# Value projection of a hybrid encoder block: the third group by seven block products, token blocks kept in place for the keys, and another order in the last row tile

## The chip, the cores and the metric

The kernel runs on one core of a Trainium2 chip, as one launch. Its time is the device time of an execution in microseconds (us); the median of the runs is compared. The engines are named as the profile names them: PE is the matrix engine (TensorE, with PEld for its weight loads), DVE the vector engine, ACT the scalar engine, POOL GpSimd, and SP the engine that issues most DMAs. ACT issues DMAs too.

## The reference

One sub-layer over 1024 tokens of 1024 channels. The input is normalised and multiplied by one wide weight matrix `w_in`; the products are the queries, keys and values of three mixers, gate paths and merge gates. The mixers' outputs are gated, projected, merged by sigmoid gates, projected once more, normalised and added to the input:

```python
h = rms_norm(x, g_pre[layer])
a_qkv, bq, bk, bv, mq, ga, gb, gm, mg = jnp.split(h @ w_in[layer], split_at, axis=-1)
a_qkv = a_qkv.reshape(b, s, 3, n_groups * A_HEADS, HEAD_DIM)
aq = rope(a_qkv[:, :, 0], pos)
ak = rope(a_qkv[:, :, 1], pos)
av = a_qkv[:, :, 2]
for gi, (window, dil) in enumerate(A_GROUPS):
    ...
out = merged @ w_out[layer]
x = x + rms_norm(out, g_post[layer])
```

`av` has 3 groups x 8 heads x 64 = 1536 columns, so each of the three value groups is a matrix product of 1024 tokens by 1024 channels by 512 columns. The keys `ak` have 1536 columns too. All of it is in float32.

## The kernel before

**Precision.** A float32 operand is split in two parts: a high part by an ACT copy into the matmul type (L105) and a low part by a DVE subtraction (L106), `split(dst_h, dst_l, src)`. A product is three matmuls: high by high, low by high, high by low. The tokens lie split in `hh` and `hl`, eight tiles of 128 channels by 1024 tokens.

**Seven block products.** Where a product can be cut into 2 x 2 blocks on both sides, the kernel takes the seven products of `PRODUCTS` in place of eight. A11, A12, A22 are blocks of weights and S1 to S4 sums and differences of them; B11, B21, B22 are blocks of tokens and T1 to T4 differences of those. T1 to T4 were formed earlier and lie unsplit in DRAM (`tsd`), four tiles of 128 x 512 each. What a product adds to which output is in the evacuation functions: S1 gives two outputs, A12 and A22 one each, the others go into running sums (`vv`, `vy`).

**The stage of the values.** Value groups VG[1] and VG[2] go together as one 1024 x 1024 x 1024 product. The loop has 28 steps, four for each of the seven products, and a step is four token tiles x three matmuls with 512 streamed columns. In a step n the loop writes down, in this order: the matmuls of n; the evacuation of one bank of the product before (`left`); the splits for step n+2 (`split_at`); sums of weights (`sum_at`); the stores of the evacuated bank; the token loads for step n+5 (`blocks_at`); and a stage of `operand`, another small job of three stages (loads, two DVE operations, a store). The third group, VG[0], follows in 16 steps of the same length as a plain product: for two token halves, eight channel tiles, four token tiles and three matmuls (the branch `i is None` at L1101). Its weights are loaded in four loads `wr<-in_wv`. During these 16 steps T1 to T4 are loaded once more from DRAM and split again, 16 tiles `kT`, for the keys. Each evacuated bank of 128 tokens x 512 columns is scaled by a column (`rcol`) and stored by ACT, operation and DMA issue (`v_store`, L948 and L949).

**The stage of the keys.** Six blocks of keys by the seven products each, 12 matmuls of 512 columns a product. The weights are loaded (`k_load`), their sums made on POOL (`k_sum`, L1039, into `sf`), and split (`k_own` for A11 and A12, `k_block` for the others, into `ch`).

**The last stage.** The output projection, again by seven products (L2019). Its last product's last bank, token tile 7, comes in two halves of 256 columns: each is summed with a running sum (L2105), squared with a row sum on ACT (L1993), added into a scalar per row (L2109) and weighted (L2110). The scalar is raised to a power on POOL (L2111), both halves of the row tile are finished (L2113) and stored by SP and ACT (L2114). `row(T)` finishes and stores another row tile (L2007, L2008).

**Order.** PE's order is written by hand in the whole kernel, and in these stages that of ACT, DVE, POOL and SP as well (`manual_schedule`): the instructions of an engine stand in the order in which the program writes them. A tile name with `bufs=n` has n places; a further tile of that name waits until the readers of the place that it takes are done.

## Time and profile before

| | us |
|---|---|
| median of 3 runs | 1418.86 (1418.45 to 1419.08) |
| the profiled execution | 1420.1 |
| its span, first to last instruction | 1418.3 |
| PE busy | 1393.4 |
| DVE busy | 1040.7 |
| ACT busy | 670.6 |
| third value group, first matmul | 538.04 |
| first matmul of the keys | 582.59 |

The mean granted clock of PE over the span is 0.998. In the profile, a row of the timeline gives the start in us from the start of the span, the duration, the engine, the line, the operation, what it writes and reads, and in brackets the idle time before it and what ended it. The duration of a matmul is longer than the distance between two of them, because they overlap; the distance is what PE needs for one. A group row gives the count, the busy time in us, the mean in ns, and idle time with what ended it. A row of the waits gives who waited for whom, the total in us, how often, and the longest. The chain is the work that ended last, followed back from the end.

### The profile page before, as it was taken

To read this page: it belongs to the slowest core of one execution; us is meant where nothing else is said; L and a number is where in the kernel's file an instruction comes from. 1 tells how busy PE (TensorE), PEld (TensorE's weight loads), DVE (VectorE), ACT (ScalarE), POOL (GpSimd) and SP (SyncE) were. 2 spreads that over 40 slices of the span, in tenths; PEclk is the share of its full clock that TensorE was granted. 3 is DMA by queue.
4 is the path that set the end of the run, shared out by engine and by line. 5 is a ranking of instruction groups with operands and counts; after the bars stand their busy time and mean duration, and the time that the engine had idled before them with its cause. 6 is when DMAs were issued, how large, how long until landed. Compare 5 with 4: busy or idle time off the path is not lost.

```text
span 1418.3 us, 21284 instructions
## 1 busy us (share of the span) xinstructions
PE 1393.4 (98%) x7496; PEld 1120.2 (79%) x7496; DVE 1040.7 (73%) x1830; ACT 670.6 (47%) x1425; POOL 505.1 (36%) x390
## 2 busy tenths in 40 slices
PE   7999999999999999999999999999999999999997
PEld 7899986656666888888888878787888888888886
DVE  7768677767773695688885777765888788677977
ACT  6544365665555445322146676656543434222232
POOL 0416703766666000432153353520433331034303
PEclk9999999999999999999999999999999999999999
DMA  6356532322210779544543554555353543856255
GB/s 238 108 166 220 182 119 71 112 82 79 75 57 23 260 225 298 162 166 178 193 131 106 129 162 116 140 140 182 106 150 126 178 171 124 321 217 212 93 199 178
DMA packets 122059, 219.67 MB, mean 155 GB/s; under 512 B 25504, under 2 KB 56032, under 8 KB 121952
## 3 DMA queue, kind: packets, MB, share of 16 engines
q1 hardware_dynamic: 95744, 187.60, 41.1%
q10 hardware_dynamic: 26208, 30.71, 6.1%
q8 instruction: 59, 0.97, 0.3%
q14 instruction: 48, 0.39, 0.1%
HBM read 152.88 MB, written 65.37 MB: 154 GB/s over the span
## 4 chain that ended last, share of the span: by engine, by line
PE 78%; DVE 6%; DMA 5%; ACT 5%; issue 3%; POOL 2%; SPq 1%; DVEq 0%; POOLq 0%; ACTq 0%
PE s L125 23%; PE sc L125 9%; PE d L143 6%; PE d L145 6%; PE d L147 6%; PE ov L803 4%; PE s L2019 3%; PE s L1101 3%; PE s L1385 2%; PE tr L1441 2%; PE s L788 2%; PE s L787 2%; PE tr L769 2%; DMA vrt<-rld 2%; PE d L544 2%
## 5 line engine op out<-in xcount | busy, mean ns | idle before, releaser
L143 PE MATMUL d<-hh,wh 128*128 128x512 f32 x480 | 194.9, 406 | 1.7 <-DVE fth L228 1.7
L145 PE MATMUL d<-hl,wh 128*128 128x512 f32 x480 | 194.1, 404 | 0.0
L147 PE MATMUL d<-hh,wl 128*128 128x512 f32 x480 | 190.7, 397 | 0.0
L794 POOL TENSOR_TENSOR bl<-bl,bp 128x512 f32<-128x512 f32 x96 | 130.7, 1362 | 54.4 <-ACT bp L790 49.0
L105 ACT ACTIVATE wh<-wr 128x512 fp32r<-128x512 f32 (+1 forms) x91 | 69.6, 772 | 133.0 <-PE sc L125 78.7
L125 PE MATMUL sc<-hh,wh 128*128 128x512 f32 x384 | 118.4, 389 | 0.0
L106 DVE TENSOR_TENSOR wl<-wr,wh 128x512 fp32r<-128x512 f32 (+1 forms) x63 | 78.9, 1265 | 50.6 <-ACT wh L105 50.6
L143 PEld LDWEIGHTS d<-hh,wh 128*128 128x128 f32 x480 | 90.3, 188 | 27.1 <-issue 6.3
L147 PEld LDWEIGHTS d<-hh,wl 128*128 128x128 f32 x480 | 90.5, 189 | 21.1 <-issue 4.7
L1398 ACT ACTIVATE pra<-pra,sts 128x192 f32<-128x192 f32 (+2 forms) x192 | 84.3, 442 | 47.9 <-DVE sts L1397 47.4
L145 PEld LDWEIGHTS d<-hl,wh 128*128 128x128 f32 x480 | 90.5, 189 | 19.2 <-issue 4.7
L790 ACT ACTIVATE bp<-s 128x512 f32<-128x512 f32 x128 | 75.7, 595 | 43.3 <-PE s L788 42.3
L770 DVE TENSOR_REDUCE bn<-tr 128x1 f32<-128x512 f32 x128 | 84.8, 683 | 12.7 <-PE tr L769 11.3
L106 DVE TENSOR_TENSOR ch<-sf,ch 128x512 fp32r<-128x512 f32 x68 | 55.9, 823 | 40.5 <-ACT ch L105 40.4
L125 PEld LDWEIGHTS sc<-hh,wh 128*128 128x128 f32 x384 | 72.1, 188 | 15.1
L105 ACT ACTIVATE ch<-sf 128x512 fp32r<-128x512 f32 x68 | 41.6, 628 | 89.3 <-PE s L125 46.4
L1249 DVE SCALAR_TENSOR_TENSOR t2a<-d,tab 32x512 f32<-32x512 f32 x96 | 66.0, 687 | 22.4 <-PE d L147 20.7
L1925 POOL TENSOR_TENSOR acc<-acc,th 128x1024 f32<-128x1024 f32 x15 | 41.3, 2756 | 109.9 <-DVE th L1924 109.9
L1039 POOL TENSOR_TENSOR sf<-wr 128x512 f32<-128x512 f32 x12 | 19.0, 1580 | 168.7 <-DMA wr<-in_wu 111.1
L1708 POOL TENSOR_TENSOR sf<-wr 128x512 f32<-128x512 f32 x22 | 28.8, 1329 | 130.4 <-DVE ch L106 81.7
L125 PE MATMUL sc<-hl,wh 128*128 128x512 f32 x192 | 74.7, 389 | 0.0
L1253 POOL TENSOR_TENSOR aq<-t1a,t2a 128x512 f32<-128x512 f32 x24 | 44.5, 1858 | 82.1 <-DVE t1a L1252 82.1
(444 smaller groups left out, 3773.9 us busy)
## 6 DMA issues: line engine op xcount, KB each, us to landing
wr<-in_wu SPq DMA_DIRECT2D x64, 512.0 KB
kd<-kr ACTq DMA_DIRECT2D x48, 256.0 KB
th<-thd SPq DMA_DIRECT2D x24, 512.0 KB
thd<-rs ACTq DMA_DIRECT2D x44, 256.0 KB
g2d<-fth SPq DMA_DIRECT2D x24, 256.0 KB
wos<-os SPq DMA_DIRECT2D x12, 512.0 KB
kraw<-kd SPq DMA_DIRECT2D x12, 512.0 KB
kswp<-kd SPq DMA_DIRECT2D x48, 128.0 KB
```

The costliest lines, as they stand in the source:

```text
L105: A.activation(dst_h, src, AF.Copy)
L106: V.tensor_tensor(dst_l, src, dst_h.bitcast(F32), op=OP.subtract)
L125: PE.matmul(out_ps, a, b, start=i == 0, stop=i == n - 1)
L143: PE.matmul(dst, wh[:, k, :], hh[k][:, t], start=k == 0, stop=False)
L145: PE.matmul(dst, wh[:, k, :], hl[k][:, t], start=False, stop=False)
L147: PE.matmul(dst, wl[:, k, :], hh[k][:, t], start=False, stop=k == 7)
L770: fp["last"] = V.tensor_reduce(st[i]["n"][:, j, c:c + 1], s, axis=AX.X, op=OP.min)
L790: A.activation(pp, s, AF.Exp, scale=-1.0)
L794: G.tensor_tensor(lsum[i % 2], lsum[i % 2], pp, op=OP.add)
L803: PE.matmul(o[e * 64:e * 64 + 64], VS[:, kt, kv], d.pop(kt), start=kt < 2, stop=kt >= NT - 2)
L1249: V.scalar_tensor_tensor(t2[i], p[j], -0.125, tab[1][j, t], op0=OP.mult, op1=OP.mult)
L1398: A.activation(src, src, AF.Exp, scale=-1.0, bias=bias, accum_out=sts[:, h, 1, T:T + 1])
```

## The change

The third group is computed by the seven products as well, cut into two halves of tokens, of channels and of columns. A matmul now streams 256 columns, two token tiles share one bank, and there are 28 steps of 12 matmuls. New functions load, sum, split, evacuate and store for it; a list `SIDE` says behind which step what is written down. A store covers 128 tokens x 256 columns, so a bank takes two of them.

The T tiles stay split through the third group and the keys: they are loaded into places of weight blocks that are done (`KT_PLACE`), the weight blocks are cut into tiles of two channel tiles each for that (`Rows`), and only two tiles of T3 are loaded and split a second time. Split weights have 2 places `sl` in place of 8 for weights and tokens together, beside `wh` and `wl`. Several tiles of the keys take places of the value stage by name.

In the last stage row 6 is finished and stored in two halves, behind the second sum of row 7's bank; the weighting of the second half moves behind the scalar.

```diff
     def split_at(i, k):
...
         if (i, k) not in SB:
-            SB[i, k] = wslot(k % 2) if i == 1 else slot()
+            SB[i, k] = wslot(k % 2 if i == 1 else 0) if i == 1 or k < 2 else slot()
...
+    KT_PLACE = {"T2": ["kT20", "kT21", "kT22", "kT23"], "T3": ["vA220", "vA221", "kT32", "kT33"],
+                "T1": ["vA110", "vA111", "vA210", "vA211"], "T4": ["vS20", "vS21", "vA120", "vA121"]}
 
     def kt_load(nm, k):
-        KT[nm, k] = tp.tile([P, 1024], R, name=f"k{nm}{k}")
+        KT[nm, k] = vb.tile([P, 1024], R, name=KT_PLACE[nm][k])
         nc.sync.dma_start(KT[nm, k][:, hi].bitcast(F32), tsd[int(nm[1]) - 1, k])
...
+    def v3_load(nm, t):
+        V3[nm] = t
+        u, kh = int(nm[1]) - 1, 4 * int(nm[2]) - 4
+        nc.sync.dma_start(t.rearrange("p (k f) -> p k f", k=4), wv[VG[0], :, kh:kh + 4, 256 * u:256 * u + 256])
+
+    def v3_sum(nm, a, b, op, t=None):
+        V3[nm] = V3[a] if t is None else t
+        V.tensor_tensor(V3[nm], V3[a], V3[b], op=op)
+
+    def v3_split(nm):
+        h, l = wslot(0), wslot(1)
+        split(h, l, V3[nm])
+        W3[nm] = [z.rearrange("p (k f) -> p k f", k=4) for z in (h, l)]
+
+    def v3_out(u, t, b, r):
+        for z in range(2):
+            T = 4 * t + 2 * b + z
+            x = r[:, half_cols[z]]
+            A.activation(x, x, AF.Copy, scale=rcol[:, T:T + 1])
+            nc.scalar.dma_start(vdr[VG[0], 2 * u:2 * u + 2, T * 128:T * 128 + 128].rearrange("p t f -> t p f"),
+                                x.rearrange("t (p f) -> t p f", p=2))
+
+    def v3_evac(i, b, ps_):
+        nm = PRODUCTS[i][0]
...
+        if nm == "A11":
+            return [lambda: A.activation(v3v[b], ps_, AF.Copy)]
+        if nm == "A12":
+            r = add(r3(), v3v[b])
+            return [lambda: v3_out(0, 0, b, r)]
+        if nm == "S1":
+            x, y = add(r3(), v3y[b]), add(v3v[b], v3v[b])
+            return [lambda: v3_out(1, 1, b, x), lambda: v3_out(0, 1, b, y)]
+        if nm == "A22":
+            y = add(v3y[b], v3y[b])
+            return [lambda: v3_out(1, 0, b, y)]
+        add((v3y if nm == "S3" else v3v)[b], v3v[b])
+        return []
...
+        if n in (16, 18):
+            v3_load(f"A1{2 if n == 16 else 1}", wp.tile([P, 1024], F32, name="wr", bufs=WR))
+        elif n in (21, 22):
+            v3_load(f"A2{n - 20}", vb.tile([P, 1024], F32, name=f"vS1{n - 21}"))
+        elif n == 24:
+            v3_split("A11")
+            kt_load("T3", 0)
+        elif n == 25:
+            v3_sum("S3", "A11", "A21", OP.subtract, V3["A21"])
+        elif n == 26:
+            v3_split("A12")
+            kt_load("T3", 1)
...
+    SIDE = {1: [lambda: operand(7, 1)],
+            2: [lambda: operand(7, 2), lambda: v3_sum("S2", "A22", "S3", OP.subtract, v3.tile([P, 1024], F32, name="xS2"))],
+            4: [lambda: v3_split("S2")], 5: [lambda: kt_split("T3", 0)], 6: [lambda: kt_split("T3", 1)],
+            8: [lambda: v3_split("S3")], 10: [lambda: v3_sum("S4", "A12", "S2", OP.subtract)], 12: [lambda: v3_split("S4")],
+            13: [lambda: k_load(0, 0)], 14: [lambda: v3_sum("S1", "A11", "S2", OP.add)], 16: [lambda: v3_split("S1")],
+            18: [lambda: k_load(0, 1)], 20: [lambda: v3_split("A22")], 23: [lambda: k_sum(0, 1)],
+            24: [lambda: k_own(0)], 25: [lambda: k_sum(0, 2)]}
+    for n in range(28):
+        i, k = divmod(n, 4)
+        an, bn = PRODUCTS[i]
+        if k == 0:
+            now = [pss1(), pss1()]
...
+        for j in range(4):
+            c = slice(j * 128, j * 128 + 128)
+            for q, (a, b) in enumerate(((bh[:, c], wh_[:, k]), (bl[:, c], wh_[:, k]), (bh[:, c], wl_[:, k]))):
+                PE.matmul(now[j // 2][:, half_cols[j % 2]], a, b, start=k == 0 and j % 2 == 0 and q == 0,
+                          stop=k == 3 and j % 2 == 1 and q == 2)
+        for _ in range(2 if n < 2 else 1):
+            for f in left.pop(0)() if left else []:
+                f()
...
+        for f in SIDE.get(n, ()):
+            f()
+        if k == 3:
+            left += [lambda i=i, b=b, z=now[b]: v3_evac(i, b, z) for b in range(2)]
 
     while left:
         for g in left.pop(0)():
             g()
...
     k_sum(0, 3)
     k_sum(0, 4)
     k_block(0, "S2")
     k_block(0, "S3")
...
-        if h == 0:
-            row(6)
+        if h:
+            row(6, (lo,))
+        else:
+            V.tensor_tensor(c11[3][:, e], vs[3][:, e], gp[:, e], op=OP.mult)
         V.scalar_tensor_tensor(r, q[:, 2 * h:2 * h + 1], 1.0 / D, r, op0=OP.mult, op1=OP.add)
-        V.tensor_tensor(c11[3][:, e], vs[3][:, e], gp[:, e], op=OP.mult)
+    V.tensor_tensor(c11[3][:, e], vs[3][:, e], gp[:, e], op=OP.mult)
+    row(6, (hi,))
     G.tensor_tensor(r, r, mhalf[:, 0:1], op=OP.pow)
```

More of the change, by code (lines that the diff above doesn't have):

```diff
@@ L1008, in kt_split @@
         split(h, l, l.bitcast(F32))
-    kt_all = [(nm, k) for nm in ("T2", "T3", "T1", "T4") for k in range(4)]
     KR = {}
@@ L1112, in block @@
             f()
[L1113 to L1120 removed]
+        if n < 23:
+            blocks_at(*divmod(n + 5, 4))
         for stage in (2, 1, 0):
@@ new lines, in block @@
+        if k == 3:
+            left += [lambda i=i, j=j, b=now[j]: v_evac(i, j, b) for j in range(4)]
+    SIDE = {1: [lambda: operand(7, 1)],
[5 more added lines that the diff above has]
+            24: [lambda: k_own(0)], 25: [lambda: k_sum(0, 2)]}
@@ L1157, in block @@
     kpp, kp = pool("kp")
-    kv_ = [kp.tile([P, 512], F32, name=f"kv{j}") for j in range(2)]
+    kv_ = [vb.tile([P, 512], F32, name=f"vv{2 + j}") for j in range(2)]
     for j in range(2):
```

117 lines of the change are left out of this document (52 added, 65 removed).

## The prediction

> **What bounds the kernel.** I read the page first, then TensorE's (PE's) waits from 455 to 600 us, the chain of waits there, and the timelines of the engines around the part that changes.
>
> ```profile
> span 1418.3 us, 21284 instructions
> ...
> PE 1393.4 (98%) x7496; PEld 1120.2 (79%) x7496; DVE 1040.7 (73%) x1830; ACT 670.6 (47%) x1425; POOL 505.1 (36%) x390
> ```
>
> ```profile
> PE s L1101 <- DVE sl L106: 0.8, 2, 0.6
> ```
>
> ```profile
> 538.04 0.39 PE L1101 MATMUL s<-wh,hh 128*128 128x512 f32 x1
> ```
>
> PE is busy for 98% of the span, so matmul time taken out is worth its full length, and a wait of PE put in costs its full length. Over this stretch PE waits hardly at all. The third value group begins at 538.04. The chain of waits shows how it runs and where it ends:
>
> ```profile
> 539.06 2.42 DMA vdr<-vr
> 541.48 0.03 issue
> 541.51 1.42 SPq L985
> 542.93 0.05 issue
> 542.98 5.05 DMA vrt<-rld
> ...
> 560.83 21.76 PE s L1101 x96
> 582.59 17.49 PE s L125 x76
> ```
>
> Ninety-six products of 512 columns take 21.76 us, 0.2267 each; the key stage begins at 582.59. The group therefore takes 44.55 us: 192 x 0.2267 = 43.5, and the rest are its waits. The first rows tell of a coupling: SP's issue of vrt waits until one of ACT's stores has landed.
>
> **What the matmuls save.** Seven block products of 48 matmuls are 336 instead of 192, each over 256 columns. Such products exist:
>
> ```profile
> 74.51 2.88 PE d L544 x24
> ```
>
> ```profile
> 96.00:108.00 12.00, 12.00 (x104) 12.00 (x103) 7.78 (x23) 4.52 (x13) 5.99 (x11) 1.00 0.29 104
> ```
>
> In the first (the chain) one takes 0.120. In the second (a table by stage: the stretch, its length, PE's busy time and matmuls) 104 touch 12 us, some 102 without the edges: 0.118. That second stage loads token weights and streams weight columns exactly as the new products do, so I take 0.118: 336 x 0.118 = 39.65, with 0.1133 (half of a 512) and 0.120 as ends (38.1 and 40.3). Against 44.55 this is **-4.9 us**, if nothing waits.
>
> The Trainium skill (TensorE: Matmul & The Clock Gate, "Back-to-back issue gap") speaks against the change: it states a sustained spacing of 81 ns for 128 columns and 131 ns for 512, so that short matmuls cost more than their share. Read linearly, 256 columns would take 98 ns, an estimate, and 336 x 98 against 192 x 131 ns is a loss of 7.7 us. The rows above, 118 against 227 ns, do not agree.
>
> **What moves to ACT and DVE.** The differences, splits and stores of the new products stand in an order written by hand, and each engine takes its work in it (I read that order from the changed kernel's own instruction lists). The prices:
>
> ```profile
> 527.84 0.68 DVE L957 TENSOR_TENSOR vr<-s,vy 128x512 f32<-128x512 f32 x1
> 528.44 0.68 DVE L957 TENSOR_TENSOR vv<-s,vv 128x512 f32<-128x512 f32 x1
> ```
>
> ```profile
> 528.56 0.72 ACT L948 ACTIVATE vr<-vr,rcol 128x512 f32<-128x512 f32 x1
> 529.32 0.37 ACTq L949 DMA_DIRECT2D vdr<-vr  x1
> 529.73 0.72 ACT L948 ACTIVATE vv<-vv,rcol 128x512 f32<-128x512 f32 x1 [0.44 <-DVE sl L106]
> ...
> 530.92 0.63 ACT L105 ACTIVATE sl<-vA 128x512 fp32r<-128x512 f32 x1 [0.47 <-ACT vv L948]
> 531.46 0.61 ACT L105 ACTIVATE sl<-sl 128x512 fp32r<-128x512 f32 x1
> ```
>
> ```profile
> L105 ACT ACTIVATE wh<-wr 128x1024 fp32r<-128x1024 f32 x31 | 32.6, 1056 | 26.3 <-DMA kd<-kr 13.7 <-PE d L145 5.4 <-ACT rs L1738 3.6
> ...
> L1398 ACT ACTIVATE pra<-pra,sts 128x256 f32<-128x256 f32 x48 | 23.8, 499 | 1.7 <-DVE sts L1397 1.6
> ```
>
> ```profile
> L518 DVE TENSOR_TENSOR wl<-wr,wh 128x1024 fp32r<-128x1024 f32 x8 | 9.8, 1223 | 1.5 <-ACT wh L517 1.4
> ```
>
> A store of 512 columns holds ACT for 1.17 (528.56 to 529.73, then 1.19), its DMA issue included; a copy 0.54, a copy of 1024 1.06. DVE steps by 0.60 for 512, takes 1.22 for 1024. A store of 256 columns is 0.50 (the row of L1398, also scaled by a column) + 0.46 = 0.96.
>
> *Into the third group.* Up to 528.56 both engines do the same work as before. That weight blocks have 4 places instead of 8 costs nothing: a place is refilled for step n+2 during step n, and its last reader was step n-2. Step 24 of the second group: two stores, then, new, the high part of A11 from 530.92 to 531.98. DVE stands at its low part until 533.2, because the adds for the next bank are behind it: adds to 534.4, the two low parts of step 27 to 535.65 (PE wants the second at 535.55; 0.1, and as much again for the first bank, which DVE frees just then: **+0.3** with its ends), the new difference S3 to 536.8. So ACT's next stores run from 533.9 to 536.25, the third pair from 537.4 to 539.8. Then A12's high part to 540.85, its low part to 542.1, and only then the fourth adds: ACT stores from 542.75 to 545.1, four of A22's to 549.75, copies a bank to 550.3, and makes S2's high part by 551.35; DVE its low part by 552.6. PE starts the group at 538.3 and, after two products of 48 x 0.118 = 5.66, wants that low part in its third matmul, at 549.9. Wait: **+2.8**. A second path says nearly the same: S2's difference stands on DVE behind the last operand, whose vrt is issued after the store of 539.35 has landed (2.42), 0.6 for the second issue, 5.05 to land: 547.4. One DVE step and a difference of 1.22 later it is 549.2, the high part 550.3, the low part 551.5: 1.6 of wait stay even with an idle ACT.
>
> Behind S2's low part DVE has two token lows and A12's add (554.4), ACT two stores of 256 (556.4), then S3's high part (557.4), DVE its low part (558.7); PE, in S2 since 552.4, wants it at 558.3: **+0.5**. S4, S1 and A22 have no such chain in front and come in time by 1 us and more. Token splits of the keys (14 pairs) go, which costs or saves nothing: they lay beside PE.
>
> *Into the keys.* Let T be the start of the last product, A22. ACT has eight stores for S1 and four for A22, in this order with the keys' own weights between:
>
> ```profile
> 585.23 1.15 ACT L105 ACTIVATE ch<-sf 128x512 fp32r<-128x512 f32 x2 [0.44 <-ACT vr L948]
> ```
>
> ```profile
> L106 DVE TENSOR_TENSOR wl<-wr,wh 128x1024 fp32r<-128x1024 f32 x1 | 2.3, 2309 | 0.0
> ```
>
> ```profile
> 569.18 1.40 POOL L1039 TENSOR_TENSOR sf<-wr 128x512 f32<-128x512 f32 x1 [111.06 <-DMA wr<-in_wu]
> ...
> 573.94 2.28 POOL L1039 TENSOR_TENSOR sf<-wr,sf 128x512 f32<-128x512 f32 x1
> ```
>
> ```profile
> 515.00:527.00 12.00, 12.00 (x55) 9.93 (x54) 11.00 (x19) 3.42 (x6) 0.00 (x0) 1.00 0.81 244
> ```
>
> Before, S2's block of the keys followed four stores at 585.23 and was in time for 588.0 (third key product). Now: first add T+0.35, four stores to T+4.2, key weights' high part T+5.2, low part T+6.4 on DVE, which PE wants at T+5.66+0.45: **+0.4**. The next adds stand behind that low part, T+7.1; eight stores to T+14.8; S2's block T+15.4, low part T+16.1. PE wants it in its third key product at T+0.4+5.66+5.44+0.45 = T+12.0: **+4.2**. Nothing after it: the four key blocks behind it are 0.6 apart, a product is 2.7.
>
> Price not shown by the trace: four weight loads of 512 KB now run between 505 and 527, where the DMA engines are busy 0.81 (last row) and DVE waits for operands. Bounds 0 and 1.5, I take +0.5: the row leaves a fifth free, and a delay moves the whole first ledger.
>
> **The last row tile.** DVE's order:
>
> ```profile
> 1409.53 0.42 DVE L2105 TENSOR_TENSOR cv<-s,cv 128x256 f32<-128x256 f32 x1
> 1410.12 0.75 DVE L2007 SCALAR_TENSOR_TENSOR xt<-cp,fss,xt 128x512 f32<-128x512 f32 x1 [0.17 <-POOL fss L130]
> ...
> 1411.85 0.42 DVE L2105 TENSOR_TENSOR cv<-s,cv 128x256 f32<-128x256 f32 x1
> 1412.90 0.16 DVE L2109 SCALAR_TENSOR_TENSOR fss<-fss 128x1 f32<-128x1 f32 x1 [0.63 <-ACT s L1993]
> ```
>
> ```profile
> 1415.29 0.37 ACTq L2114 DMA_DIRECT2D out<-xt  x1
> ```
>
> Row 6's two halves (0.75 each, from 1410.12) stand ahead of the second sum at 1411.85. With them moved behind it only a 0.42 product and a scalar that waits for ACT's square are left between the sums: the second starts at 1410.7, its scalar, as before 1.05 later, at 1411.75 instead of 1412.90. The last half of row 6 covers the power on POOL and holds row 7 for 0.2. The last store leaves 0.95 earlier; row 6 is now two stores, the second 1.3 ahead of it. **-0.9**, with 0 (the stores queue) and -1.3 as ends.
>
> **Sum.** -4.9 + 0.3 + 2.8 + 0.5 + 0.4 + 4.2 + 0.5 - 0.9 = +2.9, say **+3.0**. The profiled execution took 1420.1 (1418.3 and 1.8 around it), 1.2 above the median of 1418.86; added to that median, **1421.9**. Its own ends: 0.1133 per matmul -1.2 after S2, 0.92 or 1.0 per store -0.5 and +0.5, DMA -0.5 and +1.0, tail -0.4 and +0.9: 1420 to 1424.5.
>
> **Rivals.**
> *The stores are covered.* If ACT and DVE are never late, only -4.9 - 0.9 = -5.8 is left: 1413.1. It decides if S2's pieces are ready by 549.9 and T+12. For it speaks ACT's 47% share; against it both ledgers, where the order, not the load, sets the time. 0.08.
> *Only the keys wait.* If operands land 3 us sooner and DVE leads, the first wait goes: 1419.1. The 5.05 row speaks against it. 0.17.
> *Collisions.* POOL's four key sums reach into the key weights' low part: that row took 2309 ns beside POOL and 1223 without. With another 1.1 there, and operands 1.5 late in the first ledger: 1424.5. It decides if the keys' second weight load lands later than T-1.8, as the four sums took 7.0 (569.18 to 576.22). By the Trainium skill (GPSIMD Engine Reference, "Specifications") GpSimd and VectorE share SBUF interfaces when VectorE has two SBUF inputs; the rows agree. 0.16.
> *Short matmuls cost more than their share.* From 0.1295 each nothing is saved; at 0.140 it is +7.4 more: 1429. The two rows speak against it. 0.03.
>
> **Numbers.** Forecast 0.56. A measurement tells 0.2%, 2.8 us, from no change: under 1416.0 is faster, over 1421.7 slower. Slower: just over half of the forecast's chance, collisions and short matmuls, 0.50; faster 0.09; the rest 0.41. The range 1417.0 to 1425.5 leaves out the first and last rival and the tails.
>
> **What would show it.** In the changed profile: 336 matmuls at 0.118; PE waits of about 2.8 at the third new product, on DVE's S2 low part, and about 4 at the third key product, on DVE's low part of the first ch block; ACT storing in one run of eight before it; the last out store 0.9 nearer to the last matmul. Wrong if either wait is under 1 us, or if PE steps by over 0.125.

## The result, and the profile after

The changed kernel takes 1431.93 us, the median of four executions (1429.38 to 1432.63); the kernel before on the same chip took 1418.65 (1418.20 to 1419.08). The ratio is 1.009, with a 95% interval of 1.0073 to 1.0108. The forecast was 1421.9 with a range of 1417.0 to 1425.5: slower was right, by how much was wrong. The profiled execution of the changed kernel took 1429.38, the shortest of its four, so its profile shows about 9 of the 13 us: it lies 2.5 under its own median, and the profiled execution of the kernel before (1420.1) lies 1.5 over the median here.

The head of its page:

```profile
span 1427.4 us, 21581 instructions
## 1 busy us (share of the span) xinstructions
PE 1395.1 (98%) x7640; PEld 1125.1 (79%) x7640; DVE 1042.6 (73%) x1833; ACT 670.2 (47%) x1420; POOL 503.6 (35%) x390
```

PE's busy time hardly differs from before (1393.4), and the shares are the same. Nothing on the page says where the 9 us come from; the stages do. The table by stretch, first of the kernel before and then of the changed one: the third value group, from its first matmul to the first of the keys, and the keys up to the first matmul behind them. The columns are the stretch, its length, and the busy time and instruction count of PE, PEld, DVE, ACT and POOL, then the granted clock.

```profile
538.04:582.42 44.38, 43.81 (x193) 35.96 (x192) 21.20 (x28) 19.21 (x31) 8.04 (x5) 1.00 0.86 279
582.42:698.65 116.23, 116.23 (x506) 94.59 (x504) 94.77 (x126) 31.32 (x52) 37.24 (x22) 1.00 0.44 154
```

```profile
537.64:580.63 42.99, 40.85 (x338) 40.24 (x337) 24.38 (x32) 18.58 (x26) 5.71 (x4) 1.00 0.47 138
580.63:708.26 127.63, 120.14 (x506) 94.93 (x505) 92.84 (x126) 31.87 (x53) 37.37 (x22) 0.99 0.43 151
590.27:594.43 4.16, 4.16 (x10) 3.01 (x11) 3.17 (x5) 2.00 (x4) 0.00 (x0) 0.59 0.59 180
```

The third group is 1.4 us shorter. The keys, whose 504 matmuls the change does not touch, are 11.4 longer. The third group starts 0.4 earlier, from the keys to the last matmul it is 0.1 less, and from there to the end 0.5 less: in sum +9.05 (1418.32 to 1427.37). The last row of the table is a stretch inside the keys in which the granted clock was 0.59. No such stretch is there before.

The waits of PE in the third group, on its timeline, at the third new product:

```profile
550.59 0.50 PE L1214 MATMUL s<-wh,kT 128*128 128x256 f32 x2 [1.28 <-ACT wh L105]
551.85 0.39 PE L1214 MATMUL s<-wl,kT 128*128 128x256 f32 x1 [0.76 <-DVE wl L106]
```

The wait that was forecast is there, in the two pieces of the ledger: the high part from ACT and then the low part from DVE. From one matmul to the next it is 1.44 and 0.92 more than a step. Then the start of the keys, on ACT's timeline and below it on PE's:

```profile
581.97 0.51 ACT L1127 ACTIVATE r<-r,rcol 128x256 f32<-128x256 f32 x1 [1.89 <-DVE r L1138]
582.51 0.37 ACTq L1128 DMA_DIRECT2D vdr<-r  x1
...
588.64 0.51 ACT L1127 ACTIVATE vy<-vy,rcol 128x256 f32<-128x256 f32 x1 [0.44 <-ACT vy L1127]
589.18 0.37 ACTq L1128 DMA_DIRECT2D vdr<-vy  x1
589.59 0.63 ACT L105 ACTIVATE vS<-vot 128x512 fp32r<-128x512 f32 x1 [0.44 <-ACT vy L1127]
```

```profile
590.27 4.79 PE L125 MATMUL s<-kT,vS 128*128 128x512 f32 x12 [3.60 <-ACT vS L105]
```

Eight stores from 581.97 to 589.55, 0.95 each, and only then S2's high part: the row of stores of the forecast, with a wait of 3.76 where it had 4.2. What it did not have is in the same PE row: twelve matmuls take 4.79, while an undisturbed product takes 2.89. The low part of S2 makes 0.27 of the difference; the other 1.6 are six steps of 0.427 us and one of 0.594, in place of 0.227.

The other thing missing is further on. S1 of the second key block on ACT's timeline, before and after (these blocks start at 601.78 and 605.89):

```profile
610.29 0.63 ACT L105 ACTIVATE ch<-sf 128x512 fp32r<-128x512 f32 x1 [2.52 <-PE s L125]
```

```profile
617.13 0.63 ACT L105 ACTIVATE ch<-vot 128x512 fp32r<-128x512 f32 x1 [6.02 <-PE s L125]
...
627.35 3.45 ACTq L1087 DMA_DIRECT2D kd<-vy  x3
630.90 0.63 ACT L105 ACTIVATE ch<-vot 128x512 fp32r<-128x512 f32 x1 [7.03 <-PE s L125]
```

```profile
631.58 3.31 PE L125 MATMUL s<-kT,ch 128*128 128x512 f32 x12 [0.73 <-ACT ch L105]
```

Before, ACT writes S1 8.5 us into the block, when the third product is done; after, 11.2 us into it, when the fourth is. It waits in both for a place that PE still reads, but for another one. All that stands behind it on ACT is later by as much: the next block's own weights, its S3, the stores of rotated keys (627.35) and its S2 (630.90), for which PE now waits at 631.58. The same comes back in blocks four to six: steps of 1.1 to 1.3 in place of 0.227, and up to 0.86 for the low part.

### The profile page after: what moved, and what is told of

Its sections match the earlier page's. It is cut to its first block, busy times and chain, and to the rows that moved or that the text cites. A ratio compares the mean times of both kernels' runs of the same rounds, so it can differ in the third digit from the quotient of the medians.

```text
span 1427.4 us, 21581 instructions
## 1 busy us (share of the span) xinstructions
PE 1395.1 (98%) x7640; PEld 1125.1 (79%) x7640; DVE 1042.6 (73%) x1833; ACT 670.2 (47%) x1420; POOL 503.6 (35%) x390
## 4 chain that ended last, share of the span: by engine, by line
PE 78%; DVE 7%; ACT 5%; DMA 5%; POOL 2%; issue 2%; SPq 1%; ACTq 1%; DVEq 0%; POOLq 0%
PE s L125 21%; PE sc L125 9%; PE d L143 6%; PE d L145 6%; PE d L147 6%; PE s L2098 4%; PE ov L803 3%; PE s L1463 2%; PE tr L1519 2%; DMA vrt<-rld 2%; PE s L788 2%; PE s L787 2%; PE tr L769 2%; PE d L544 2%; PE d L2098 2%
## 5 line engine op out<-in xcount | busy, mean ns | idle before, releaser
L105 ACT ACTIVATE wh<-wr 128x512 fp32r<-128x512 f32 (+1 forms) x93 | 72.6, 788 | 135.3 <-PE sc L125 75.3
L106 DVE TENSOR_TENSOR wl<-wr,wh 128x1024 fp32r<-128x1024 f32 (+1 forms) x67 | 82.3, 1240 | 61.5 <-ACT wh L105 61.5
L1786 POOL TENSOR_TENSOR sf<-wr 128x512 f32<-128x512 f32 x22 | 29.8, 1373 | 131.6 <-DVE ch L106 69.4
L1052 POOL TENSOR_TENSOR vot<-wr 128x512 f32<-128x512 f32 x6 | 10.8, 1805 | 178.1 <-DMA wr<-in_wu 113.3
L1816 ACT ACTIVATE rs<-rs,hbm 128x512 f32<-128x512 f32 x44 | 31.7, 721 | 76.4 <-DVE rs L1815 75.8
L1394 POOL TENSOR_TENSOR ak<-kraw,kswp 128x512 f32<-128x512 f32 x24 | 48.0, 2027 | 54.2 <-DMA avs<-vdr 18.9
```

The lines of the kernel that those rows point to most:

```text
L105: A.activation(dst_h, src, AF.Copy)
L106: V.tensor_tensor(dst_l, src, dst_h.bitcast(F32), op=OP.subtract)
```

## The experiments

The expectations count the key blocks from zero where they give them numbers (blocks 2 to 5 are the third to the sixth); the text here counts from one. Every time is set against the kernel before on the same chip. In the tables "group" is the third value group and "keys" the key stage, as in the table by stretch; the kernel before has 44.39 and 116.23, the changed one 42.99 and 127.63. The softmax stage is what follows the keys, up to the same matmul in every kernel, the one that starts at 1071.32 in the profile of the kernel before (372.67 there, 372.38 in the changed kernel).

**The turn of the places, in both kernels.** The split weight blocks of the keys had four places of one name before. In the changed kernel the same four blocks of memory have names, taken in turn. In the first run they go by block:

```diff
-        x = next(ch_turn) % 4
+        x = {"S2": 0, "S1": 0, "S3": 1, "A22": 2, "S4": 3}[nm]
```

> The changed kernel with one difference: the split weight blocks of the keys take their four places by name (S1 always the place of S2; S3, A22 and S4 one each) and not in turn. In turn, S1 of a key block stands in the place of S3 of the same block, so ACT cannot write it before the fourth key product is done; in the kernel before it is written when the third is done, 2.7 us earlier in its block (8.50 against 11.24), and on ACT the next block's own weights, its S3 and its S2 stand behind it. Theory 1 (the turn of the places makes the waits at the third product of key blocks 2 to 5): S1 is written 8.5 us into its block, the four waits of 0.9 to 1.9 are gone, the key stage takes 127.6 - 5.9 = 121.7 us and the kernel 5.9 us less than the changed one, a profiled span of about 1421.5. Rival (DVE, the shared places of the running rows, or POOL's sums make them): waits and time stay within 1 us. The 3.8 us wait in key block 0 stays under both.

In the second run the kernel before gets the turn:

```diff
-        t = kp.tile([P, 1024], R, name="ch", bufs=4)
+        t = kp.tile([P, 1024], R, name=f"ch{next(ch_turn) % 4}")
```

> The kernel before with one difference: the split weight blocks of the keys stand in four named places taken in turn, as in the changed kernel. Theory 1 (the turn alone makes the waits of key blocks 2 to 5): S1 is written when the fourth product of its block is done, waits of about 1 us appear at the third product of blocks 2 to 5, and the kernel takes 4 to 6 us more than the one before, a profiled span of 1422 to 1424. Rival (it needs the other moves of the change): no wait and no difference over 1 us.

The first has 1425.86 (ratio 1.0043, 1.0029 to 1.0057) and keys of 121.34, 6.3 less than the changed kernel; the four late waits are gone. The second has 1424.16 (1.0034, 1.0021 to 1.0047) and keys of 121.41, 5.2 more than before; waits stand at the third product of the third to the sixth block:

```profile
PEld s L125 <- ACT ch L105: 4.8, 4, 1.2
PEld s L125 <- DVE ch L106: 1.7, 4, 0.4
```

So the turn alone, with nothing else of the change, costs the keys 5.2 us, and without it the changed kernel gets 6.3 back. This part is shown from both sides. Why a name with four places let S1 follow S2 and not S3 was not looked into; that it did, the row at 610.29 shows.

**S2 ahead of the stores.** The first key block's S2 is split ahead of the second half of S1's stores:

```diff
-            24: [lambda: k_own(0)], 25: [lambda: k_sum(0, 2)]}
+            24: [lambda: k_sum(0, 2), lambda: k_own(0), lambda: k_block(0, "S2")]}
```

> The changed kernel with one difference: the split of the first S2 block of the keys, with the sum that it needs, is written behind the keys' own weights, ahead of the second half of S1's stores and of A22's stores. Theory 1 (ACT's row of eight stores holds the third key product): its wait of 3.76 us goes; the fourth product then waits for S3, whose split is still behind the stores: ready at about 590.1 against 589.2 wanted, 0.9 to 1.5 us. As no wait of over 3 us is left, the nine steps of 0.427 us behind it (1.9 us) go as well. Time 4 to 4.8 us under the changed kernel, profiled span about 1423. Rival (the slow steps come from the operands of that product or from the transfers beside it, not from the idle time ahead of them): the steps stay at 0.427 and only 2.3 to 2.9 us are gained, a span of about 1425. The waits of key blocks 2 to 5 stay under both.

1430.81 (1.008, 1.0065 to 1.0095): a median 1.1 less, where over 4 was expected. The keys are 2.2 shorter (125.47): the 3.76 and the slow steps are gone, and the wait at the fourth product, 1.93, is longer than expected. But the third group is 44.06, 1.1 longer, though nothing in it was changed, and the softmax stage 2.0 longer, so that the whole profile is 1.8 us over that of the changed kernel. The clock by stretch, in the third group behind the two waits, and in the keys behind the 1.93:

```profile
551.80:556.00 4.20, 3.43 (x15) 3.22 (x16) 3.03 (x4) 2.18 (x5) 0.00 (x0) 0.61 0.03 7
592.00:598.00 6.00, 4.57 (x19) 3.43 (x20) 4.36 (x7) 3.87 (x7) 0.00 (x0) 1.00 0.61 191
```

The slow steps of this execution are in the third group.

**One store less to wait for.**

```diff
-            return [lambda: v3_out(1, 0, b, y)]
+            if b:
+                return [lambda: v3_out(1, 0, b, y, (0,)), lambda: k_block(0, "S2"), lambda: v3_out(1, 0, b, y, (1,))]
+            return [lambda: v3_out(1, 0, b, y)]
```

> The changed kernel with one difference: the first S2 block of the keys is split ahead of the last of the eight stores instead of behind it, so that the wait ahead of the third key product is one store (0.96 us) shorter, 2.8 us in place of 3.76. Theory 1 (a wait of over some 3 us makes TensorE restart at about half its rate, for 4 us): at 2.8 us the nine steps of 0.427 us become 0.227, and the time falls by 0.96 + 1.9 = 2.9 us, a profiled span of 1424.5; the executions also lie closer together than the 3.2 us of the changed kernel. Rival (the slow steps belong to that product, whatever waits ahead of it): the time falls by 0.96 alone, a span of 1426.4.

```profile
589.06 4.82 PE L125 MATMUL s<-kT,vS 128*128 128x512 f32 x12 [2.67 <-ACT vS L105]
```

1433.22 (1.0095, 1.008 to 1.011). The wait is 2.83, as built; the slow steps stayed (seven of 0.427). My threshold of some 3 us was wrong. The keys are 127.35, only 0.3 less and not 0.9, as a low part in the fourth block came 0.5 later (a step of 1.39 in place of 0.86); the median is higher, with a softmax stage of 374.5 in place of 372.4 in the profile. For the rival speaks that the slow steps stayed, so the next run takes the idle time itself away.

**Matmuls in place of the wait.** On the kernel with places by block:

```diff
+            if (n, i) == (0, 1):
+                warm = terms
+            if (n, i) == (0, 2):
+                passes(dst, warm + warm[:2])
             passes(dst, terms)
```

> The kernel with weight blocks by name (first of these runs) with one difference: while TensorE would wait for the third key product of the first block it does 14 matmuls of the product before once more, into the bank that the third product then overwrites (3.2 of the 3.76 us). Nothing is ready earlier. Theory 1 (TensorE falls to half its rate through the idle time itself): the wait left is about 0.6 us, no step of 0.427 us follows it, the granted clock stays at 1.00 from 590 to 595 us, and the time falls by 1.9 to 2.5 us. Rival (the steps are slow through the operands of that product or the transfers at that time): the steps stay at 0.427 and the time is the same.

The same stretch without the added matmuls (the first kernel) and with them:

```profile
590.00:595.00 5.00, 4.37 (x12) 3.15 (x13) 3.19 (x5) 2.62 (x5) 0.00 (x0) 0.71 0.69 223
```

```profile
590.00:595.00 5.00, 4.14 (x17) 2.83 (x16) 1.72 (x3) 3.67 (x8) 1.45 (x1) 1.00 0.71 211
```

With PE kept busy the clock stays at 1.00, and no step of 0.427 is there, with the same operands and like transfers beside them (DMA share 0.69 and 0.71). The idle time makes the slow steps: this is shown, by one profile of each kernel. A wait of 1.02 is left, 0.4 more than expected. The keys are 120.19 against 121.34, 1.2 less and not 1.9: the slow steps of the first kernel's profile cost 1.6, and S2 came 0.4 later after the start of the keys. The whole kernel was not faster (1427.90; 1.0048, 1.0033 to 1.0064): in its profile the slow steps are in the third group, and the softmax stage took 378.0 us, more than in any other profile. (It was also the longest of that kernel's five executions.)

**The changed kernel again.**

> The changed kernel once more, for its own spread: its profiled execution was 2.5 us under its median. Theory 1 (half-rate steps follow the waits of the third group in some executions and that of the keys in others, or both): the profile shows such steps at one of the two places or both, and the executions spread over 3 us, while those of a kernel without long waits spread over 2. Rival (the spread comes from the later stage with the softmax, where the kernel before too waits 1 to 3 us): the steps are the same as in the first profile and the difference lies behind 708 us.

1433.13 (1.0103, 1.0087 to 1.0118).

```profile
589.77 5.49 PE L125 MATMUL s<-kT,vS 128*128 128x512 f32 x12 [3.89 <-ACT vS L105]
```

Here the slow stretch is longer: the keys take 129.29, 1.7 more than in the first profile. The softmax stage takes 374.9 in place of 372.4. With a third group that is 0.6 shorter and 0.4 less in the rest, that is the 3.15 us by which this span is the longer one; both theories hold a part of it. The four executions spread over 2.25 us, not 3.

**The last row tile alone, on the kernel before** (the diff of the last stage as in the change):

> The kernel before with the new order of the last row tile alone. Forecast of the sum: the last store is issued 0.9 us nearer to the last matmul, and the time falls by 0.9. From the changed kernel's profile: the store is issued 1.05 nearer, but from the last matmul to the end it is 8.35 in place of 8.83, so 0.5 less. Rival (the two stores of row 6 that now stand just ahead of the last one take the gain back): no change within 0.2 us of the profile's end, the store landing later by what it was issued earlier.

1418.26 against 1419.34 (0.9990, 0.9981 to 0.9999), 1.1 less. From the last matmul to the end it takes 1.1 less as well. The forecast term of -0.9 holds here, the rival does not.

**Taking the waits away one after the other.** Each row is the kernel above with a further edit, C and D with several:

| kernel | edit | group | keys | longest waits left | ratio (95% interval) |
|---|---|---|---|---|---|
| A | places by name, S2 and S3 early | 44.22 | 118.32 | 1.49 + 0.91 group, 1.37 keys | 1.0022 (1.0013-1.0031) |
| B | two stores behind S2 | 44.74 | 118.23 | 1.45 + 0.92 group, 1.33 keys | 1.0026 (1.0017-1.0035) |
| C | four steps moved | 40.88 | 122.72 | 2.80 + 1.79 keys | 1.0027 (1.0016-1.0039) |
| D | stores issued by SP, a load earlier | 40.93 | 120.14 | 2.99 keys | 1.0013 (1.0004-1.0022) |
| E | POOL's table product later | 40.65 | 120.53 | 3.40 keys | 1.0015 (1.0006-1.0024) |
| F | S2 earlier, second block | 40.91 | 119.01 | 1.86 keys | 0.9988 (0.9979-0.9997) |
| G | the third block too | 40.96 | 117.87 | 1.60 + 0.91 keys | 0.9998 (0.9988-1.0008) |
| H | all blocks | 40.78 | 115.36 | 0.39 group | 0.9987 (0.9978-0.9996) |

A:

```diff
+        x = {"S2": 0, "S1": 0, "S3": 2, "A22": 1, "S4": 3}[nm]
...
+            24: [lambda: k_sum(0, 2), lambda: k_sum(0, 3), lambda: k_own(0), lambda: k_block(0, "S2"), lambda: k_block(0, "S3")]}
```

> The changed kernel with the two repairs for the keys together: weight blocks by name (S1 in the place of S2, one place each for S3, A22 and S4), and the sums and splits of both S2 and S3 of the first key block ahead of S1's second four stores and A22's four. Theory 1 (the price of the change lies in these two places of the key stage, and the slow steps of 0.427 us follow from the long wait): the waits of key blocks 2 to 5 (5.9), the wait of 3.76 and the slow steps (1.9) go together, the key stage takes 116 us as in the kernel before, and the profiled span is 1427.4 - 11.5 = 1416, its median about 3 us under that of the kernel before. Rival (the stores only move, and hold another step of the keys, A22's or S4's split): one of the products 4 to 7 of the first block waits 1 us or more and the median is not under that of the kernel before.

(S3 is split ahead of the stores as well here, and S3 and A22 have exchanged their places.) The keys lose 9.3 of their 11.4. The third group is in its slow form (44.22, fourteen steps of 0.21 in place of 0.12). A new wait of 1.37 is in the second key block, and SP's queue shows why:

```profile
SPq L1240 <- DMA vdr<-r: 11.2, 1, 11.2
```

SP's load of the table stands until stores have landed (11.2), and the second block's weights stand behind it: asked for at 590.03 in place of 577.61 before. In the changed kernel they are asked for at 586.86, and the wait of 3.76 hid that.

B:

```diff
-                f()
+                f() if n != 1 else late.append(f)
...
+        if n == 4:
+            for f in late:
+                f()
```

> The kernel of the run before in this row (both repairs of the keys) with one more: in the third value group the last two stores of the second group stand on ACT behind the split of S2 and not ahead of it. Theory 1 (that wait is ACT's row of stores, as forecast): the two waits at the third new product fall from 1.44 and 0.92 to about 0.4 together, the group takes 40.7 us in place of 43, and as its cold steps cannot follow either the median falls by 2 to 3 us more, to about 5 under the kernel before. Rival (S2's difference comes late through the last operand, the second path of the forecast): at least 1.5 us of the wait stay.

S2's wait falls from 2.4 to 0.5, but 1.45 and 0.92 come at S3, which now stands behind the moved stores and A12's. The same time, with half-rate steps behind it as in A: a wait moved by one product.

C splits S3 one step earlier, S4 of the first key block ahead of A22, the keys' own weights ahead of S1's stores, and loads the second block's first weights ahead of the table:

> All repairs so far (weight blocks by name; S2 and S3 of the first key block ahead of the stores; two stores of the second group behind S2's split in the third group), and what stood late in the profiles of those kernels: the third group's S3 is split one step earlier, ahead of A12's stores (it waited 1.45 and 0.92 behind them); in the first key block S4 is split before A22 (S4 was 0.5 late); the keys' own weights are split ahead of S1's stores (0.3); and the weights of the second key block are asked for ahead of the two loads of the table, behind which SP held them until 590.0 in place of 577.6 (S2 of the second block was 1.4 late). Theory 1 (all that the change lost is waits in an order of hand-written queues, and cold steps that follow them; the block products themselves save their 4.9): the third group takes about 40.5 us, the key stage about 116.5, no step runs at half rate, and the median is 4 to 5 us under the kernel before, a ratio of 0.997. Rival (each repair moves the wait to the next block, as it did in the third group): at least 2 us of waits are found in other products of these stages, and the ratio is 0.999 or more.

The group is at 40.88 with one wait of 0.48. The keys are worse: they start 4.2 us earlier than in A, but the stores end only 1.4 earlier, at 591.4, and S4 stands behind them:

```profile
PEld s L125 <- ACT ch L105: 3.1, 1, 3.1
PEld s L125 <- DVE ch L106: 2.1, 1, 2.1
```

D:

```diff
-            nc.scalar.dma_start(vdr[VG[0], 2 * u:2 * u + 2, T * 128:T * 128 + 128].rearrange("p t f -> t p f"),
+            (nc.sync if u or t else nc.scalar).dma_start(vdr[VG[0], 2 * u:2 * u + 2, T * 128:T * 128 + 128].rearrange("p t f -> t p f"),
...
+            24: [lambda: k_sum(0, 2), lambda: k_sum(0, 3), lambda: k_block(0, "S2"), lambda: k_block(0, "S3"), lambda: k_load(1, 0)]}
...
-    k_load(1, 0)
```

> The kernel of the run before in this row with one more difference: the DMAs of S1's and A22's stores in the third group are issued by SP and not by ACT (0.42 of the 0.96 us that a store of 256 columns holds ACT), with the second key block's first weights ahead of the later ones. In the profile of that kernel the third group took 40.9 us, but S4 of the first key block, behind eight stores, came 2.8 us late, its low part ran 2.32 us beside POOL and cost 1.8 more, and cold steps followed. Theory 1 (ACT's queue at the start of the keys is the one place left): ACT reaches S4's split at about 588.2, the key product that needs it begins at 589.3, no step over 0.6 us is left from 580 to 610, the key stage takes 116.5 to 117.5 us, and the median is 3 to 4 us under the kernel before (ratio 0.997 to 0.998). Rival (SP becomes the late one: a store waits for its lane and the table or the next weights come late): a wait of 1 us or more in the first or second key block, and a ratio of 0.999 or more.

The first key block has no wait any more; S2 of the second has one of 2.99, with slow steps. As the rival had it, the table came late on SP's queue (asked for at 586.71, in C at 579.56).

E moves POOL's product on the table behind its sums:

> The kernel of the run before in this row with POOL's product on the table moved behind its four sums for the second key block. There the first key block had no wait left, but the table, whose load now stands behind the stores on SP, came so late that POOL's product ran from 593.0 to 595.4, ahead of the sums; S3 of the second block was split at 600.3, and its S2 came 3.0 us late with cold steps behind it (3.0 + 1.8). Theory 1 (that is the last place): POOL's sums begin at about 592.5, S2 of the second block is ready in time, the key stage takes 115.5 to 116.5 us, no step runs at half rate, and the median is 3.5 to 5 us under the kernel before (ratio about 0.997). Rival (the weights, not POOL, hold the sums, as both come through the same queue): S2 of the second block still waits 1 us or more and the ratio stays at or over 1.

It then ran beside DVE's rotation of the keys. The rows of POOL and DVE:

```profile
597.90 2.85 POOL L1282 TENSOR_TENSOR tab<-tab,rb 128x1024 f32<-128x1024 f32 x1
```

```profile
598.41 2.89 DVE L1084 TENSOR_TENSOR vy<-vy,tab 128x512 f32<-128x512 f32 x1
601.40 0.69 DVE L1085 TENSOR_TENSOR vy<-vy,tab 128x512 f32<-128x512 f32 x1
```

A DVE operation of about 0.7 takes 2.89 while POOL's runs, as the low part in the prediction took 2.31 beside POOL, and ACT's stores wait for the rotation. The wait is longer, 3.40.

F (DVE takes the product on the table, and S2 of the second block is split at `i == 5` of the first), G and H (`if n < 2 and i == 5`, then `n < 5`):

> The kernel of the run before in this row with two differences in the first key block: DVE and not POOL takes the table's second product (POOL's ran 2.85 us beside DVE's, which took 2.89 in place of 0.7), and S2 of the second block is split one product earlier, ahead of two of the four stores of rotated keys that held ACT until 605.6. Theory 1 (the waits are the whole loss, and an order without them exists): the second block's third product starts without a wait, the key stage takes 116 to 117 us, no step at half rate is left, and the median is 3 to 4 us under the kernel before, a ratio of 0.997 to 0.998. Rival (with the block products ahead of it, the start of the keys has too little time for its loads and splits in any order): a wait of over 1 us stays somewhere in the first two key blocks and the ratio is 0.999 or more.

> The kernel of the run before in this row with S2 of the third key block, too, split one product earlier. There the first two key blocks ran without a wait and the median fell under that of the kernel before; S2 of the third block was 1.86 us late, as its stores of rotated keys still ran behind, and seven steps at half rate followed. Theory 1 (an order without waits exists): the last wait goes with its slow steps, the key stage takes 115.5 to 116.5 us in place of 119.0, and the ratio is 0.996 to 0.998. Rival (the lag moves on, as it did from the first block to the third): a wait of over 1 us in the fourth block, with or without slow steps, and a ratio that stays at 0.999.

> As the run before in this row, with S2 of every key block split one product earlier. There the wait moved on to the fourth block (1.6 and 0.9 us): S1 of each block was still written 11.8 us into the block in place of 8.5, because ACT's stores of rotated keys run 3 us behind from the first block on, and blocks 2 and 3, whose S2 stood ahead of those stores, had no wait all the same. Theory 1 (an order without waits exists): with S2 ahead of them everywhere the lag costs nothing, the key stage takes 115.0 to 115.8 us, and the ratio is 0.996 to 0.998. Rival (the lag has to come out somewhere): a wait of over 1 us at another product, or behind the keys before 720 us, and a ratio of 0.999 or more.

In F and G the wait moves on by one block each time; the rival of G is met: there it is in the fourth block. H has none. The table by stretch, and all of PEld's waits from 537 to 694:

```profile
538.24:579.02 40.78, 40.55 (x338) 40.16 (x336) 25.46 (x32) 18.78 (x28) 5.07 (x4) 1.00 0.42 128
579.02:694.37 115.35, 115.35 (x506) 94.61 (x505) 93.38 (x125) 30.32 (x51) 34.07 (x21) 1.00 0.51 172
```

```profile
PEld s L1215 <- DVE wl L106: 0.6, 2, 0.4
PEld s L125 <- DVE wl L106: 0.4, 1, 0.4
```

1418.08 against 1419.47: 0.13% (0.04 to 0.22) faster than the kernel before, with the block products, the kept token blocks and the last row tile of the change, and another order. The keys came out as expected (115.0 to 115.8), the ratio of 0.996 to 0.998 did not. And the last row tile alone gave 0.10% (0.01 to 0.19): that the block products and the kept blocks gain anything in the whole time is not shown by these medians.

**Where the rest of the gain goes.** H finishes the keys 4.3 us earlier than the kernel before in its profile, and the tail saves 0.8 more, but the median is 1.4 under. The softmax stage takes 376.30 in H and 372.67 before. A second profile of both:

> The kernel before once more, for the stage behind the keys (softmax, 698.65 to 1071.32, 372.7 us in its first profile). Theory 1 (that stage varies from one execution to the next whatever comes ahead of it): it takes anything from 372.4 to 375. Rival (it is the same in every execution of the same code): 372.7 within 0.3.

> The kernel without waits in the third group and the keys once more, for the same stage, which took 376.3 us in its first profile. Theory 1 (the stage varies by chance): it takes 372.4 to 375 us this time. Rival (the stage is bound by DVE and ACT from its start, so that what the keys finish earlier is given back there): 375.5 to 377 us again.

372.95 for the kernel before, which fits both expectations, and 374.79 for H, which is within what chance was given and under the rival's 375.5. Both profiles of H lie over both of the kernel before, by 1.8 to 3.6. PE's waits in it, from 715 to 1000 us, in the second profile of the kernel before and then of H:

```profile
PE tr L1415 <- ACT app L1427: 1.1, 2, 0.7
PE tr L1441 <- ACT app L1427: 0.8, 1, 0.8
PE tr L1424 <- ACT og L1449: 0.4, 1, 0.4
```

```profile
PE tr L1494 <- ACT app L1506: 1.7, 2, 0.8
PE s L1464 <- DVE sts L1476: 0.8, 1, 0.8
PE tr L1520 <- ACT app L1506: 0.8, 1, 0.8
PE tr L1503 <- ACT og L1528: 0.4, 1, 0.4
```

H waits 1.4 us more there, for DVE and ACT. That a part of the gain is given back where DVE and ACT set the pace fits this, but it is not shown: the stage took 374.7 with the last row tile alone changed, 372.4 and 374.9 in two profiles of the changed kernel, and 378.0 in the kernel with matmuls in place of the wait, none of which finishes the keys more than 1.3 us ahead of the kernel before.

## Why the prediction was wrong, step by step

**What held.** The cause named for the two forecast waits was right: the order of ACT's and DVE's work, not PE. Every sign that the prediction named for itself was there, and the time was wrong all the same: none of these signs looked at the keys behind the first block.

- Matmuls: the price of 0.118 was 0.119 (mean of the steps without a wait in H's group), 40.0 in place of 39.65. (The group before took 44.39, not 44.55: the keys' first matmul starts at 582.42, and the 582.59 of the chain is where a piece of the chain begins. So -4.9 was 0.2 too much, and with 0.119 it is -4.4.) The rival of short matmuls that cost more than their share is out. By the spacing that the Trainium skill states (TensorE: Matmul & The Clock Gate, "Back-to-back issue gap") they would have cost 7.7 us more, an estimate; the trace does not agree.
- First ledger: 2.8 forecast, 1.44 + 0.92 = 2.36 measured (0.78 + 0.92 in the second profile), ACT's high part and DVE's low part as said; 0.5 for S3, 0.26 measured. Of the 0.3 at its start and the 0.5 for added loads nothing is seen: the group starts 0.4 earlier, and its start lies anywhere from 536.83 to 538.24 in the profiles of kernels that have the old code up to there. As a whole it gains 1.4 where the terms gave 0.8.
- Second ledger: 4.2 at the third key product, 3.76 measured, and 0.27 behind it for the low part; 0.4 for the keys' own low part, 0.30 measured.
- Tail: -0.9, measured -1.1 by itself; in both profiles of the changed kernel the stretch behind the last matmul is only 0.5 shorter. Why was not looked into.

**What failed** is a step that was one clause: "Nothing after it: the four key blocks behind it are 0.6 apart, a product is 2.7." It looked at one key block only, and at splits, not at the places they go into. The change to places taken in turn was in the diff, and the text ahead of the prediction says that tiles of the keys take places by name; the prediction does not ask who still reads the place that S1 takes, and so puts the blocks behind the first at nothing. The price is 6.3 us (127.63 to 121.34 without the turn). The row that would have given it stood in the profile of before, the wait of S1 for PE at 610.29: the prediction quotes no row of blocks 2 to 6.

**The second missing term** is PE's rate after a wait. The sum took a wait of 4.2 as 4.2. It cost 1.6 more in the first profile and 3.0 in the second, through steps of 0.427. The Trainium skill states that rule on the page that the prediction cites for another (TensorE: Matmul & The Clock Gate, "Part 1: The HAM clock gate"): after an idle window of some 3.4 us the clock falls to half, and a busy one brings it back. By its number the forecast waits (2.8, and 4.2 in the keys) would have called for a term in the keys. The trace agrees on the half (0.427 against 0.227, granted clock 0.50) and on a window of 3.41 us, but the window ahead of the fall was not idle throughout: see below.

In the sum of the profiled execution the keys are +11.4 where the terms gave +4.6; the 6.8 between them are these two, 6.3 and 1.6, less 1.1 for terms that came out smaller and for steps of the key stage that are shorter in all kernels of the new form (115.36 in H, without waits, against 116.23). The medians lie another 4 us apart: 1.5 of it is the profiled execution of the kernel before, and 2.5 that of the changed kernel, whose second profile is longer by the slow stretch and the softmax stage.

Of the rivals, "collisions" named 1424.5 for POOL beside DVE and late operands: not what happened in the changed kernel, though it came when the waits ahead of it were gone (kernels C to E). The bounds were the other error: each unknown got ends of half a microsecond around a ledger that left out whole steps, so the range could not hold them. (Added up plainly, the ends listed under the sum give 1419.3 to 1424.3, not 1420 to 1424.5.)

## What to carry to other kernels

When tiles move from one name with several places to names taken in turn, write down for each tile whose place it takes and when the last reader of that is done, through a full period: a wait behind the first block costs once per block. A wait of PE of some 2 us or more can bring a half-rate stretch of 3.41 us behind it, or two; that cost 1.6 and 3.0 us here, and as its length differs from one execution to the next, it also spreads the times. Where queues are ordered by hand, a saved wait shows the next one in line: here it took eight kernels until 115.4 us of keys stood without a wait, and the whole time then gained little more than the last row tile gives alone.

## What the runs showed of the hardware

PE fell to half its rate after waits shorter than expected, and not always. With half-rate steps behind them: 4.05, 3.76 (twice), 3.40, 2.99 and 2.83 us; 2.80 with 1.79 in C; 1.86 in F; 1.50 with 0.92 in the group of the kernel with S2 early, of A and of the kernel with matmuls in place of the wait; and 1.44 with 0.92 in B. Without: 1.93 at the fourth key product with S2 early, 1.60 with 0.91 in G, the same 1.44 with 0.92 in the first profile of the changed kernel, and 1.51 with 0.92 in the first kernel with places by block. So the length of the wait alone does not decide it.

The granted clock in the traces says more. In each of the 12 falls in the third group or the keys it was 0.50 for 3.41 us, or for twice that (in C and in the second profile of the changed kernel), whatever the wait. Cut into stretches of 3.41 us, counted from the edges of the fall in the same profile, the group of A reads:

```profile
549.27:552.68 3.41, 1.33 (x10) 0.92 (x8) 1.30 (x2) 2.97 (x6) 0.00 (x0) 1.00 0.66 185
552.68:556.09 3.41, 3.41 (x16) 3.41 (x17) 1.73 (x3) 1.21 (x3) 0.00 (x0) 0.50 0.05 16
```

The same wait in the first kernel with places by block, where it has no half-rate steps behind it:

```profile
547.70:551.11 3.41, 2.06 (x17) 1.86 (x16) 0.23 (x1) 2.53 (x4) 0.00 (x0) 1.00 0.98 272
551.11:554.52 3.41, 2.65 (x22) 2.45 (x21) 2.79 (x4) 1.77 (x4) 0.00 (x0) 1.00 0.03 8
```

In A nearly the whole wait lies in one stretch, and PE is busy for 1.33 us of it; here a boundary of the grid cuts it in two. In all 12 falls PE was busy for 1.76 us or less of the stretch ahead; in the stretches with the waits that had no fall behind them, for 1.64 (the 1.93), 1.8 (G) and 1.9 or more. The two ranges overlap a little, so PE's busy time is not the whole rule; but where a wait lies on this grid counts beside its length. This is read from the profiles; no run moved a wait to test it.

An order edit in which the kernel's own arithmetic stays the same can move half-rate steps to another stage: with S2 early the keys gained 2.2 us, and the third group, in which nothing was changed, lost 1.1 against the first profile of the changed kernel.
